# Layer 0's feed-forward with both residual streams in DRAM and its down sums added there by accumulating DMAs

## The chip, the cores and the metric

The kernel runs on one core of one Trainium2 chip. The metric is the device time of one execution in microseconds (us); the median of three plain runs before the change is 3101.7 us. A core has TensorE (PE, matrix products into PSUM), VectorE (DVE), ScalarE (ACT), GpSimd (POOL) and SyncE (SP, which here only issues DMAs), each working through its own instructions in order, and 16 DMA engines that they share. "PEld" is PE's loading of weights.

## The reference

Two layers act on two streams of 256 tokens by 2048 channels in float32: a latent stream `h` and a context stream `hc`. Layer 0 mixes by centred pooling, layer 1 by neighbourhood attention; each is followed by a gated feed-forward of width 5504. What matters here is layer 0, where both streams are updated:

```python
def conv_ffn(u, w_gate, w_up, conv_w, conv_b, w_down):
    T = u.shape[1]
    gp = jnp.pad(u @ w_gate, ((0, 0), (1, 1), (0, 0)))
    gte = gp[:, :T] * conv_w[0] + gp[:, 1:T + 1] * conv_w[1] + gp[:, 2:] * conv_w[2] + conv_b
    return (jax.nn.silu(gte) * (u @ w_up)) @ w_down
...
        h = h + ml[:, 2] * y_lat
        h = h + ml[:, 5] * conv_ffn(modulate(rms_norm(h, norm2_g[i]), ml[:, 3], ml[:, 4]),
                                    ffn_w_gate[i], ffn_w_up[i], ffn_conv_w[i], ffn_conv_b[i], ffn_w_down[i])
        if not last:
            hc = hc + mc[2] * y_ctx
            hc = hc + mc[5] * conv_ffn(modulate(rms_norm(hc, norm2_g[i]), mc[3], mc[4]),
                                       ffn_w_gate[i], ffn_w_up[i], ffn_conv_w[i], ffn_conv_b[i], ffn_w_down[i])
```

`ml` and `mc` are per-layer shifts, scales and gates, products of `silu(c)` and `silu(c_ctx)` with `w_mod`.

## The kernel before

**Layout.** Channels stand on the 128 partitions: a stream is 16 tiles (`KT`) of 128 channels by 256 tokens (`T`). The latent stream is `hl`, which lives for the whole kernel; the context stream is `hc`, 16 KB per partition, which lives until layer 0 ends. Each product is taken in three passes with the operands split in a high and a low part: ACT makes the high part (L143), DVE subtracts (L145), and PE runs hi x hi, hi x lo and lo x hi over 512 columns, both streams side by side.

**Mixer, up to some 455 us.** `mixer(g)` handles four tiles of channels. POOL adds the mixed result into `hl` and `hc` (L493); after group `g` these tiles of the streams are final until the feed-forward's own sums. The layer's modulation weights `wm` go through PE here (L193) in six slots, and the first eight feed-forward columns are computed group by group (`partial`, weights `wcg` and `wcu`).

**Feed-forward of layer 0, some 455 to 1694 us.** The 43 hidden tiles form eleven groups (`chunks`) of four, the last of three. For a hidden tile `f`, `gu0(f)` is 2 x 48 products over weights `wg_f` and `wu_f` (each loaded in two halves of 512 KB), and `gate0` makes the activation. For a group `c`, `down0(c)` is 16 tiles of 12 products each into the PSUM banks with tag "d" (three, and one with tag "m"); it follows the gate/up products of the next group. ACT scales each result by the gate into a buffer `dy` (L669, once for each stream) and POOL adds it to the stream (L670). Only in the last group DVE adds it, and the norm of the next layer is gathered there. Weights come by SP: three slots of 512 KB, then four pairs of high and low parts, so a half is asked for some seven halves ahead of its use. Between them SP loads layer 1's modulation weights (L219, L223), on which DVE works beside (`mod_pairs`, L241) in three slots of their own.

**Order.** Tiles come from pools, and a tile's reuse waits for its earlier readers. The framework orders each engine's instructions by a timeline that it simulates while it builds the program, so an edit can move instructions far from where it is written. Instructions on one engine, DMAs on SP's and on POOL's queue included, run in that order: one that waits holds up all behind it.

Of the kernel before, what the change touches and what calls it, by code (L numbers as in the profile page):

```python
# [10 lines left out]
F32 = mybir.dt.float32  # L11
F32R = mybir.dt.float32r
AF = mybir.ActivationFunctionType
ALU = mybir.AluOpType
# [3 lines left out]
P = 128  # L18
D = 2048
KT = D // P  # L20
T = 256
# [36 lines left out]
def kernel(ctx: ExitStack, tc: tile.TileContext, xT, cxT, wmod, wg, wu, wd, wp,  # L58
                         wq, wv, wo, vec, cc, rope, inv, strips, out):
    nc = tc.nc  # L60
# [8 lines left out]
    def bank(tag, name):  # L69

        if tag == "d" and nbank[0] is not None:
            nbank[0] += 1
            if nbank[0] % 4 == 0:
                tag = "m"
        return pp.tile([P, 512], F32, tag=tag, bufs={"gu": 4, "d": 3, "m": 1}[tag], name=name)

    def flat(a):
        return a.rearrange("p s t -> p (s t)")
# [5 lines left out]
    def V(name):  # L84
        a, b = _OFF[name]
        return vt[:, a:b]
# [11 lines left out]
    hl = main.tile([P, KT, T], F32, name="hl")  # L98
# [50 lines left out]
    def ld(src, name, share=0):  # L149
        return split(load(lambda a, b: src[:, a:b], 2048, name), name, share)  # L150
# [4 lines left out]
    both = (0, 1)  # L155
# [105 lines left out]
    def M(l, which, k, s):  # L261
        return modT[l, which * 4 + k // 4][:, k % 4, s : s + 1]
# [41 lines left out]
    def normalise(l, which, h_of, streams, rstd, pool, ks=range(KT), keep=A):  # L304

        for k in ks:
            a = ap0.tile([P, 2, 2, T], F32R, tag=f"A{k}", name=f"A{k}_{l}_{which}")
            y = pool.tile([P, 2, T], F32, tag="t2", name=f"nrm{l}{which}{k}")
            for s in streams:
                nc.vector.scalar_tensor_tensor(y[:, s], h_of(s)[:, k, :], M(l, which + 1, k, s),  # L310
                                               rstd[:, T * s : T * s + T], op0=ALU.mult, op1=ALU.mult)
                nc.scalar.activation(a[:, 0, s, :], y[:, s], AF.Identity, bias=M(l, which, k, s))
                ins = nc.vector.scalar_tensor_tensor(a[:, 1, s, :], y[:, s], M(l, which, k, s),
                                                     a[:, 0, s, :].bitcast(F32), op0=ALU.add, op1=ALU.subtract)
            keep[k] = a
            if l == 1 and k == 1:
                hold[:] = [ins.ins]

    chunks = [list(range(f, min(f + 4, NF))) for f in range(0, NF, 4)]
# [3 lines left out]
    with ExitStack() as ph0:  # L323
        p0 = ph0.enter_context(tc.tile_pool(name="p0", bufs=1, reuse_waits="tile"))
        f0 = ph0.enter_context(tc.tile_pool(name="f0", bufs=6, reuse_waits="tile"))
        hc = p0.tile([P, KT, T], F32, name="hc")

        quad = p0.tile([P, 4, 32], F32, name="quad")
        nc.vector.tensor_reduce(out=quad[:, 0], in_=ident.rearrange("p (j c) -> p c j", j=4), axis=AX.X, op=ALU.add)
# [2 lines left out]
        quad = flat(quad)  # L332

        def h_of(s):
            return hc if s else hl

        def act_tile(name, dt):
            return f0.tile([P, 2, 512], dt, tag="act", bufs=7, name=name)
# [23 lines left out]
        def gate0(f, pg, pu):  # L362
            g1 = f0.tile([P, 2, T], F32, tag="t2", name=f"g1_{f}")
            nc.scalar.activation(flat(g1), pg, AF.Identity, scale=V("cw1_0")[:, f : f + 1], bias=V("cb_0")[:, f : f + 1])
            pg3 = pg.rearrange("p (s t) -> p s t", s=2)
            nc.vector.scalar_tensor_tensor(g1[:, :, 1:T], pg3[:, :, 0 : T - 1], V("cw0_0")[:, f : f + 1],
                                           g1[:, :, 1:T], op0=ALU.mult, op1=ALU.add)
            nc.vector.scalar_tensor_tensor(g1[:, :, 0 : T - 1], pg3[:, :, 1:T], V("cw2_0")[:, f : f + 1],
                                           g1[:, :, 0 : T - 1], op0=ALU.mult, op1=ALU.add)
            sg = f0.tile([P, 512], F32, tag="t2", name=f"sg_{f}")  # L370
            nc.scalar.activation(sg, flat(g1), AF.Silu)
            nc.vector.tensor_tensor(sg, sg, pu, op=ALU.mult)
            if f == NS - 1:
                a = mp.tile([P, 2, 512], F32R, tag="macc", bufs=1, name=f"act_{f}")
            else:
                a = act_tile(f"act_{f}", F32R)
            a = [a[:, 0], a[:, 1]]
            nc.scalar.copy(a[0], sg)
            nc.vector.tensor_tensor(a[1], sg, a[0].bitcast(F32), op=ALU.subtract)
            return a, sg  # L380
# [5 lines left out]
        with ExitStack() as phs:  # L386
            st = phs.enter_context(tc.tile_pool(name="st", bufs=2, reuse_waits="tile"))
            for g in range(4):
                nc.sync.dma_start(hl[:, 4 * g : 4 * g + 4, :], xT[:, 4 * g : 4 * g + 4, :])
                nc.sync.dma_start(hc[:, 4 * g : 4 * g + 4, :], cxT[:, 4 * g : 4 * g + 4, :])  # L390
            n1 = Norm(both, f0, "n1")
            for k in range(KT):
                n1.add(h_of, k)
# [226 lines left out]
        def gu0(f):  # L620
            res = []
            for nm, wsrc in (("g", wg), ("u", wu)):
                parts = ld(wsrc[0, f], f"w{nm}0_{f}")
                if f > NS + 3:
                    next(pump, None)
                ps = bank("gu", f"{nm}0_{f}")
                for k in range(KT):
                    hi, lo = parts[k // 8]
                    c = P * (k % 8)
                    xh, xl = flat(A[k][:, 0]), flat(A[k][:, 1])  # L630
                    nc.tensor.matmul(ps, hi[:, c : c + P], xh, start=(k == 0), stop=False)  # L631
                    nc.tensor.matmul(ps, hi[:, c : c + P], xl, start=False, stop=False)  # L632
                    nc.tensor.matmul(ps, lo[:, c : c + P], xh, start=False, stop=(k == KT - 1))  # L633
                    if k == 7 and f > NS + 3:
                        next(pump, None)
                res.append(ps)
            return res
# [3 lines left out]
        def down0(c, fs, acts, after=None):  # L641
            n = len(fs)
            last = c == len(chunks) - 1
            for mg in range(4):
                parts = split(load(lambda a, b: wd[0, mg, :, fs[0] + a // 512 : fs[0] + b // 512, :], 512 * n, f"wd0_{c}_{mg}"),
                              f"wd0_{c}_{mg}")
                if c > 1:
                    next(pump, None)
                for m in range(4):
                    if m == 2 and c > 1:  # L650
                        next(pump, None)
                    ps = bank("d", f"d0_{c}_{mg}_{m}")
                    for i in range(n):
                        hi, lo = parts[i // 2]
                        o = 512 * (i % 2) + P * m
                        xh, xl = acts[i]
                        nc.tensor.matmul(ps, hi[:, o : o + P], xh, start=(i == 0), stop=False)  # L657
                        nc.tensor.matmul(ps, hi[:, o : o + P], xl, start=False, stop=False)  # L658
                        nc.tensor.matmul(ps, lo[:, o : o + P], xh, start=False, stop=(i == n - 1))  # L659
                    k = 4 * mg + m  # L660
                    if last:
                        for s in both:
                            nc.vector.scalar_tensor_tensor(h_of(s)[:, k, :], ps[:, T * s : T * s + T], M(0, 5, k, s),
                                                           h_of(s)[:, k, :], op0=ALU.mult, op1=ALU.add)
                        n3.add(h_of, k)
                    else:
                        y = f0.tile([P, 2, T], F32, tag="t2", name=f"dy{c}_{k}")
                        for s in both:
                            nc.scalar.activation(y[:, s], ps[:, T * s : T * s + T], AF.Copy, scale=M(0, 5, k, s))  # L669
                            nc.gpsimd.tensor_tensor(h_of(s)[:, k, :], h_of(s)[:, k, :], y[:, s], op=ALU.add)  # L670
                if after is not None:
                    after()
# [2 lines left out]
        normalise(0, 3, h_of, both, rstd, f0, range(12, 14))  # L675
        acts[NC], sg = gate0(NC, *r6)
        normalise(0, 3, h_of, both, rstd, f0, range(14, KT))
        res = gu0(NS)
        rest = [e for e in range(NS) if e not in acts]

# [5 lines left out]
        while rest and rest[0] < 4:  # L686
            more()
        down0(0, chunks[0], [acts[f] for f in chunks[0]], more)
        while rest:
            more()  # L690
        acts[NS], sg = gate0(NS, *res)
        for c, fs in enumerate(chunks):
            if c < 2:
                continue
            fs = [f for f in fs if f > NS]
            for f in fs:
                acts[f], sg = gate0(f, *gu0(f))
            down0(c - 1, chunks[c - 1], [acts[f] for f in chunks[c - 1]])
        prev = (len(chunks) - 1, chunks[-1], [acts[f] for f in chunks[-1]])
        down0(*prev)  # L700
        for _ in pump:
            pass
# [529 lines left out]
```

## Time and profile before

| what | value |
|---|---|
| median of three plain runs | 3101.7 us (3101.54 to 3102.39) |
| the profiled execution | 3103.48 us, its span 3101.7 us |
| granted TensorE clock over the span | 0.993 |
| DMA | 559.70 MB, 180 GB/s over the span |
| written to DRAM | 2.10 MB |

The profile is of one execution. Its page gives the busy time of each engine, the chain of work that ended last, followed back from the last instruction to whatever released each step, and groups of instructions by line, operation and tile: busy time, mean time of one, and the idle time of the engine just before them with what ended it. Other views list waits, instructions in order of time, and busy time by stretches. PE's products overlap, so the duration of one (0.395 us) is longer than the distance from one to the next.

### The profile page before, as it was taken

What the parts mean: (1) busy time and instruction counts of PE and PEld (TensorE: products, weight loads), DVE (VectorE), ACT (ScalarE), POOL (GpSimd) and SP (SyncE); (2) the same over time, 40 slices, a digit from 0 to 9 for tenths busy, and PEclk for the clock granted to TensorE, in tenths of its full rate; (3) what the DMA queues carried; (4) which work ended last, traced back from release to release, by engine and by line L of the source; (5) the groups of instructions that cost most, each with busy time, mean ns of one, the idle gap of its engine ahead of it and who ended that gap; (6) DMA issues with size and microseconds to landing.
All of it is one profiled execution on the core that took longest, in us unless ns stands there. A gap on an engine that the chain in (4) does not pass through costs nothing.

```text
span 3101.7 us, 40819 instructions
## 1 busy us (share of the span) xinstructions
PE 3030.0 (98%) x15082; PEld 2414.3 (78%) x15082; DVE 1932.6 (62%) x2748; ACT 1373.2 (44%) x2219; POOL 826.1 (27%) x823
## 2 busy tenths in 40 slices
PE   6999899999999999999999999999999999999998
PEld 2565558888888888888888788878788888888887
DVE  4445674285765848567485665564777666666666
ACT  3333454333233332323334444343545666656665
POOL 2011213213031230302213000000002466556665
PEclk9999999999999999999999999999999999999999
DMA  9978573264846657475573333332345565555563
GB/s 376 333 271 306 177 246 102 89 217 149 251 141 206 198 162 247 133 225 171 182 226 118 102 113 106 102 114 96 111 153 179 177 196 188 192 189 185 179 195 117
DMA packets 177927, 559.70 MB, mean 180 GB/s; under 512 B 17600, under 2 KB 22208, under 8 KB 177728
## 3 DMA queue, kind: packets, MB, share of 16 engines
q1 hardware_dynamic: 177728, 557.10, 55.0%
q8 instruction: 119, 1.95, 0.3%
q14 instruction: 80, 0.66, 0.1%
HBM read 554.93 MB, written 2.10 MB: 180 GB/s over the span
## 4 chain that ended last, share of the span: by engine, by line
PE 94%; DMA 2%; DVE 2%; POOL 1%; ACT 1%; issue 0%; SPq 0%; DVEq 0%; ACTq 0%; POOLq 0%
PE g L766 5%; PE u L766 5%; PE d L657 5%; PE d L659 5%; PE d L658 5%; PE d L813 4%; PE u L631 4%; PE u L632 4%; PE u L633 4%; PE g L631 4%; PE g L633 4%; PE g L632 4%; PE mod L193 3%; PE u L769 3%; PE g L769 3%; PE d L817 2%
## 5 line engine op out<-in xcount | busy, mean ns | idle before, releaser
L670 POOL TENSOR_TENSOR hl<-hl,dy 128x256 f32<-128x256 f32 x160 | 149.0, 931 | 958.6 <-ACT dy L669 957.3
L828 POOL TENSOR_TENSOR hl<-hl,dy 128x256 f32<-128x256 f32 x320 | 331.5, 1069 | 188.4 <-ACT dy L826 186.1
L241 DVE SCALAR_TENSOR_TENSOR macc<-wm,sc,macc 128x512 f32<-128x512 f32 (+1 forms) x360 | 325.2, 935 | 68.6 <-DMA wm<-wmod 67.6
L669 ACT ACTIVATE dy<-d,modT 128x256 f32<-128x256 f32 x320 | 133.5, 470 | 196.8 <-PE d L659 195.5
L193 PE MATMUL mod<-wm,sc 128*32 128x512 f32 x768 | 134.6, 618 | 26.6 <-DMA wm<-wmod 26.5
L670 POOL TENSOR_TENSOR hc<-hc,dy 128x256 f32<-128x256 f32 x160 | 126.0, 787 | 0.0
L145 DVE TENSOR_TENSOR wd_2l<-wd,wd_2h 128x1024 fp32r<-128x1024 f32 (+1 forms) x44 | 53.9, 1229 | 112.8 <-ACT wd_2h L143 112.8
L826 ACT ACTIVATE dy<-d,modT 128x512 f32<-128x512 f32 x160 | 104.4, 683 | 42.7 <-PE d L817 41.2
L915 POOL TENSOR_TENSOR rk<-rk,rp 128x256 f32<-128x256 f32 x16 | 13.2, 826 | 365.4 <-DVE rk L914 309.8
L145 DVE TENSOR_TENSOR wd_3l<-wd,wd_3h 128x1024 fp32r<-128x1024 f32 (+1 forms) x44 | 52.0, 1202 | 80.6 <-ACT wd_3h L143 80.6
L145 DVE TENSOR_TENSOR wd_1l<-wd,wd_1h 128x1024 fp32r<-128x1024 f32 (+1 forms) x44 | 53.7, 1224 | 58.6 <-ACT wd_1h L143 58.6
L466 POOL TENSOR_TENSOR pf<-ws,inv 128x256 f32<-128x256 f32 x32 | 27.7, 886 | 222.4 <-DVE ws L461 154.7
L193 PEld LDWEIGHTS mod<-wm,sc 128*32 128x32 f32 x768 | 23.6, 110 | 81.0 <-issue 59.4
L143 ACT CAST wd_1h<-wd 128x1024 fp32r<-128x1024 f32 (+1 forms) x44 | 45.2, 1029 | 79.8 <-PE u L632 50.6
L145 DVE TENSOR_TENSOR wd_0l<-wd,wd_0h 128x1024 fp32r<-128x1024 f32 (+1 forms) x44 | 54.6, 1247 | 40.7 <-ACT wd_0h L143 40.6
L1004 ACT ACTIVATE sb<-sb,nm 128x512 f32<-128x512 f32 x64 | 46.1, 721 | 64.4 <-DVE nm L1000 63.2
L143 ACT CAST wd_0h<-wd 128x1024 fp32r<-128x1024 f32 (+1 forms) x44 | 45.3, 1031 | 57.9 <-PE u L766 29.1
L792 DVE TENSOR_TENSOR actb<-sgb,actb 128x256 fp32r<-128x256 f32 x43 | 52.3, 1216 | 27.0 <-ACT actb L791 27.0
L657 PE MATMUL d<-act,wd_2h 128*128 128x512 f32 x172 | 68.0, 395 | 0.0
L658 PE MATMUL d<-act,wd_2h 128*128 128x512 f32 x172 | 67.9, 395 | 0.0
L657 PE MATMUL d<-act,wd_3h 128*128 128x512 f32 x172 | 67.9, 395 | 0.0
L657 PE MATMUL d<-act,wd_0h 128*128 128x512 f32 x172 | 67.9, 395 | 0.0
(1752 smaller groups left out, 9286.1 us busy)
## 6 DMA issues: line engine op xcount, KB each, us to landing
wm<-wmod SPq DMA_DIRECT2D x384, 512.0 KB, 6.1
wd<-wd SPq DMA_DIRECT2D x168, 512.0 KB, 4.4
wg<-wg SPq DMA_DIRECT2D x156, 512.0 KB, 4.6
wu<-wu SPq DMA_DIRECT2D x156, 512.0 KB, 4.5
wv<-wv SPq DMA_DIRECT2D x32, 512.0 KB, 3.9
wk<-wq SPq DMA_DIRECT2D x32, 512.0 KB, 4.0
wq<-wq SPq DMA_DIRECT2D x32, 512.0 KB, 3.7
wo<-wo SPq DMA_DIRECT2D x32, 512.0 KB, 4.4
```

The lines of the kernel that those rows point to most:

```text
L145: eng.tensor_tensor(lo[:, :n], t[:, :n], hi[:, :n].bitcast(F32), op=ALU.subtract)
L193: nc.tensor.matmul(ps[32 * j : 32 * j + 32, :], sc[:, 4 * g + j, :], ts[j // 2][0][:, 512 * (j % 2) : 512 * (j % 2) + 512], start=(g == 0) ...
L241: nc.vector.scalar_tensor_tensor(acc[s], v, sc2[:, k, s : s + 1], acc[s], op0=ALU.mult, op1=ALU.add)
L631: nc.tensor.matmul(ps, hi[:, c : c + P], xh, start=(k == 0), stop=False)
L632: nc.tensor.matmul(ps, hi[:, c : c + P], xl, start=False, stop=False)
L633: nc.tensor.matmul(ps, lo[:, c : c + P], xh, start=False, stop=(k == KT - 1))
L657: nc.tensor.matmul(ps, hi[:, o : o + P], xh, start=(i == 0), stop=False)
L658: nc.tensor.matmul(ps, hi[:, o : o + P], xl, start=False, stop=False)
L670: nc.gpsimd.tensor_tensor(h_of(s)[:, k, :], h_of(s)[:, k, :], y[:, s], op=ALU.add)
L766: nc.tensor.matmul(ps, hi[:, c : c + P], flat(B[k]), start=(k == 0), stop=False)
L769: nc.tensor.matmul(ps[:, T:], lo[:, c : c + P], B[k][:, 0], start=False, stop=(k == KT - 1))
L828: nc.gpsimd.tensor_tensor(hl[:, k, :], hl[:, k, :], y[:, q], op=ALU.add)
```

## The change

- A DRAM tile `hd` holds both streams. `moved(True)`, in the program after the second norm, stores `hl` and `hc` there by eight DMAs of 512 KB on SP's queue.
- The room of `hc` is then used as `dys`, eight slots of one down tile of both streams each (256 KB).
- In `down0` of groups 0 to 8, ACT writes the scaled results to a slot of `dys`, and in place of POOL's two adds one DMA on POOL's queue adds the slot to `hd` in DRAM: 144 such DMAs, each of 256 rows of 1 KB.
- After the gate of hidden tile 40 the room becomes a context stream again (`hc2`), and `moved(False)` loads both streams back by eight DMAs of 512 KB. Groups 9 and 10 are added on chip as before.

```diff
+        dr = ph0.enter_context(tc.tile_pool(name="dr", bufs=1, space=bass.MemoryType.DRAM))
+
+        hd = dr.tile([P, 2, KT, T], F32, name="hd")
+        CTX = [p0.tile([P, KT, T], F32, tag="hc", name="hc")]
...
         def h_of(s):
-            return hc if s else hl
+            return CTX[0] if s else hl
...
+                    elif away:
+                        y = away[0][:, 2 * (k % 8) : 2 * (k % 8) + 2, :]
+                        for s in both:
+                            nc.scalar.activation(y[:, s], ps[:, T * s : T * s + T], AF.Copy, scale=M(0, 5, k, s))
+                        nc.gpsimd.dma_start(out=hd[:, :, k, :], in_=y, accum_op=ALU.add)
                     else:
                         y = f0.tile([P, 2, T], F32, tag="t2", name=f"dy{c}_{k}")
...
         normalise(0, 3, h_of, both, rstd, f0, range(14, KT))
+
+        def moved(out_):
+            for g in range(0, KT, 4):
+                for s in both:
+                    x, y = hd[:, s, g : g + 4, :], h_of(s)[:, g : g + 4, :]
+                    if out_:
+                        nc.sync.dma_start(x, y)
+                    else:
+                        nc.sync.dma_start(y, x)
+
+        moved(True)
+        away = [p0.tile([P, KT, T], F32, tag="hc", name="dys")]
         res = gu0(NS)
...
                 acts[f], sg = gate0(f, *gu0(f))
+                if f == fs[0] and c == len(chunks) - 1:
+                    away.clear()
+                    CTX[0] = p0.tile([P, KT, T], F32, tag="hc", name="hc2")
+                    moved(False)
             down0(c - 1, chunks[c - 1], [acts[f] for f in chunks[c - 1]])
```

Three places in the order of the instructions. The first is SP's queue near the end of the mixer's stage, with modulation weights `wm_15` and `wm_20` of layer 0 and hidden weights `wcu`. Before:

```order
L127 DMA wm_15_2_1024_2845<-wmod 128x1024
L127 DMA wm_15_3_0_2865<-wmod 128x1024
L127 DMA wm_15_3_1024_2867<-wmod 128x1024
L127 DMA wm_20_1_0_2951<-wmod 128x1024
L127 DMA wm_20_1_1024_2953<-wmod 128x1024
```

And in the changed kernel, at the same place:

```order
L127 DMA wm_15_2_1024_2848<-wmod 128x1024
L692 DMA hd<-hl 128x1024
L127 DMA wm_15_3_0_2868<-wmod 128x1024
L127 DMA wm_15_3_1024_2870<-wmod 128x1024
L692 DMA hd<-hc 128x1024
L127 DMA wm_20_1_0_2954<-wmod 128x1024
L127 DMA wm_20_1_1024_2956<-wmod 128x1024
```

The stores of the last four tiles of each stream stand ahead of loads of modulation weights; the other three pairs stand in the same way after their mixer groups.

The second place is SP's queue around the ninth group's down products, with the weights of hidden tiles 40 and 41 and the modulation weights of layer 1 (`wm_7`, `wm_22`). Before:

```order
L127 DMA wd_8_3_1024_11732<-wd 128x1024
L127 DMA wg_40_0_11827<-wg 128x1024
L127 DMA wg_40_1024_11829<-wg 128x1024
L127 DMA wu_40_0_11915<-wu 128x1024
L127 DMA wu_40_1024_11917<-wu 128x1024
L127 DMA wg_41_0_11998<-wg 128x1024
L219 DMA wm_7_3_11885<-wmod 128x1024
L127 DMA wg_41_1024_12000<-wg 128x1024
L127 DMA wu_41_0_12071<-wu 128x1024
L219 DMA wm_7_4_11927<-wmod 128x1024
L127 DMA wu_41_1024_12073<-wu 128x1024
```

And in the changed kernel, from `wu_40` on:

```order
L127 DMA wu_40_0_11639<-wu 128x1024
L694 DMA hl<-hd 128x1024
L127 DMA wu_40_1024_11641<-wu 128x1024
L127 DMA wg_41_0_11731<-wg 128x1024
L694 DMA hl<-hd 128x1024
L127 DMA wg_41_1024_11733<-wg 128x1024
L127 DMA wu_41_0_11804<-wu 128x1024
L694 DMA hc_11722<-hd 128x1024 x3
L694 DMA hl<-hd 128x1024
L694 DMA hc_11722<-hd 128x1024
L127 DMA wu_41_1024_11806<-wu 128x1024
```

The reloads stand among the weights, five of them just ahead of the second half of `wu_41`; the loads of `wm_7` that stood here have moved ahead of `wg_40`. The reloads of `hl` each wait for the accumulations of their four tiles, the first of `hc` for all of the ninth group's.

The third place is the end of the mixer's stage on PE, around the last quarter of the products with `wm_15`. Before, these rows follow `wm_15_2_1024`:

```order
L289 MATMUL n2s<-ones,n2q_2749 128x1 x2
L545 MATMUL cg_0_2836<-Ad_2795,wcg_0h_2828 128x512
L545 MATMUL cg_1_2858<-Ad_2795,wcg_0h_2828 128x512
L193 MATMUL mod_15_2767<-wm_15_3_0_2865,sc 32x512 x2
L546 MATMUL cg_0_2836<-Ad_2795,wcg_0h_2828 128x512
```

In the changed kernel the same product stands behind twelve more:

```order
L549 MATMUL cg_1_2861<-Ad_2817,wcg_0h_2831 128x512
L550 MATMUL cg_1_2861<-Ad_2817,wcg_0l_2832 128x512
L548 MATMUL cg_0_2839<-Ad_2822,wcg_0h_2831 128x512
L548 MATMUL cg_1_2861<-Ad_2822,wcg_0h_2831 128x512
L193 MATMUL mod_15_2770<-wm_15_3_0_2868,sc 32x512 x2
L549 MATMUL cg_0_2839<-Ad_2822,wcg_0h_2831 128x512
```

What moved is only the place of the product with `wm_15_3_0`: the `cg` products that came after it now come ahead of it.

More of the change, by code (lines that the diff above doesn't have):

```diff
@@ L325 @@
         f0 = ph0.enter_context(tc.tile_pool(name="f0", bufs=6, reuse_waits="tile"))
-        hc = p0.tile([P, KT, T], F32, name="hc")
+        dr = ph0.enter_context(tc.tile_pool(name="dr", bufs=1, space=bass.MemoryType.DRAM))
+        hd = dr.tile([P, 2, KT, T], F32, name="hd")
+        CTX = [p0.tile([P, KT, T], F32, tag="hc", name="hc")]
         quad = p0.tile([P, 4, 32], F32, name="quad")
@@ L389 @@
                 nc.sync.dma_start(hl[:, 4 * g : 4 * g + 4, :], xT[:, 4 * g : 4 * g + 4, :])
-                nc.sync.dma_start(hc[:, 4 * g : 4 * g + 4, :], cxT[:, 4 * g : 4 * g + 4, :])
+                nc.sync.dma_start(CTX[0][:, 4 * g : 4 * g + 4, :], cxT[:, 4 * g : 4 * g + 4, :])
             n1 = Norm(both, f0, "n1")
```

## Prediction

> **What bounds the kernel now.** I read the page's first part and its chain first, then busy time by stage.
>
> ```profile
> PE 3030.0 (98%) x15082; PEld 2414.3 (78%) x15082; DVE 1932.6 (62%) x2748; ACT 1373.2 (44%) x2219; POOL 826.1 (27%) x823
> PE 94%; DMA 2%; DVE 2%; POOL 1%; ACT 1%; issue 0%; SPq 0%; DVEq 0%; ACTq 0%; POOLq 0%
> ```
>
> PE is busy for 98% of the span and makes up 94% of the chain that ended last; POOL, whose work the change takes away, makes up 1%. The stages (the columns are the stretch, its length, then busy time and instructions of each engine, the granted clock, the DMA share and GB/s):
>
> ```profile
> 0.00:30.00 30.00, 10.26 (x42) 4.78 (x42) 11.71 (x25) 12.11 (x34) 4.10 (x15) 1.00 0.92 345
> 30.00:455.00 425.00, 401.81 (x2142) 226.80 (x2141) 226.31 (x397) 164.33 (x299) 72.84 (x77) 0.98 0.79 285
> 455.00:1694.00 1239.00, 1239.00 (x5415) 1014.01 (x5414) 773.94 (x971) 448.26 (x698) 268.26 (x320) 1.00 0.56 176
> ...
> 770.00:847.00 77.00, 77.00 (x339) 63.29 (x339) 64.93 (x82) 21.60 (x25) 0.00 (x0) 1.00 0.83 259
> 847.00:924.00 77.00, 77.00 (x338) 62.89 (x337) 43.11 (x59) 30.07 (x50) 26.76 (x32) 1.00 0.41 130
> ...
> 1517.00:1562.00 45.00, 45.00 (x196) 36.51 (x195) 14.88 (x17) 21.02 (x39) 23.98 (x30) 1.00 0.30 99
> ```
>
> The stage that the change rewrites, layer 0's feed-forward from 455 to 1694 us, has PE busy for all of its 1239 us. A busy PE need not be at its peak, so I compare counts: 339 products in 77 us without any POOL work and with the DMA share at 0.83, 338 with 26.76 us of POOL work and the share at 0.41. So neither POOL's adds nor DMA traffic up to 0.83 changes PE's pace of 77/338 = 0.228 us for a product. There is nothing to win in this stage, only something to lose. What PE waited for in the two stages:
>
> ```profile
> PE g L631 <- DVE late L355: 0.9, 1, 0.9
> ...
> PE modt L203 <- ACT modev L198: 7.8, 7, 1.6
> PE mod L193 <- DMA wm<-wmod: 6.8, 11, 2.8
> PE pwu L528 <- DMA wcu<-wu: 5.4, 2, 4.1
> ```
>
> The first row is all that PE waited for from 455 to 1694 us (0.9 us, at its start); the other three are the largest waits of the mixer's stage, 30 to 455 us. There PE idled 425 - 401.8 = 23.2 us, of which 6.8 + 5.4 = 12.2 us were for loads. It is the only place where the new order could gain anything.
>
> **The adds on POOL go.** Nine groups by 16 tiles by two streams: 288 of these 320 instructions.
>
> ```profile
> L670 POOL TENSOR_TENSOR hl<-hl,dy 128x256 f32<-128x256 f32 x160 | 149.0, 931 | 958.6 <-ACT dy L669 957.3
> L670 POOL TENSOR_TENSOR hc<-hc,dy 128x256 f32<-128x256 f32 x160 | 126.0, 787 | 0.0
> L669 ACT ACTIVATE dy<-d,modT 128x256 f32<-128x256 f32 x320 | 133.5, 470 | 196.8 <-PE d L659 195.5
> ```
>
> That is 144 x (0.931 + 0.787) = 247 us of POOL time, but POOL idled 957 us there waiting for ACT, and ACT for PE. Gain on the path: **0**. ACT's two evictions per tile stay, into another buffer: 0.
>
> **The 144 accumulating DMAs.** No row shows one, so I bound the pace t, the time from the end of one to the end of the next.
>
> ```profile
> wd<-wd SPq DMA_DIRECT2D x168, 512.0 KB, 4.4
> wd<-wd SPq DMA_DIRECT2D x8, 256.0 KB, 2.7
> q1 hardware_dynamic: 177728, 557.10, 55.0%
> ```
>
> A load of 256 KB lands in 2.7 us and one of 512 KB in 4.4: 1.7 us for each 256 KB more, and 1.0 us that does not grow. From below, t = 1.7 us, if the add is free. From above by packets: 0.550 x 3101.7 x 16 / 177728 = 0.154 us of one engine for each packet of some 3 KB. The new DMA has 256 rows of 1 KB; if each row costs three packets (source read, destination read, write), t = 768 x 0.154 / 16 = 7.4 us; with two, 4.9. I take **3.4 us**, the 256 KB load's price with the bytes counted twice, as the row nearest to it.
>
> What t has to stay under: the pitch of the tiles.
>
> ```profile
> 1517.75 0.40 PE L657 MATMUL d<-act,wd_0h 128*128 128x512 f32 x1
> ...
> 1520.75 0.84 ACT L669 ACTIVATE dy<-d,modT 128x256 f32<-128x256 f32 x2 [1.97 <-PE d L659]
> 1523.55 0.84 ACT L669 ACTIVATE dy<-d,modT 128x256 f32<-128x256 f32 x2 [1.96 <-PE d L659]
> ```
>
> The ninth group's down product begins at 1517.75, and a tile is evicted every 2.80 us. POOL's queue then holds nothing but these DMAs, each waiting for its eviction and for the landing of the eighth before it; ACT waits for that same landing before it writes a slot again, and behind it stand the weight casts on which PE depends. The 16th tile, evicted at 1520.75 + 15 x 2.80 = 1562.8, needs the 8th DMA, done at 1521.6 + 8t + 1.0; the four banks of PSUM give three tiles more, 8.4 us. So ACT stops PE only when t > (1562.8 + 8.4 - 1522.6)/8 = **6.1 us**. At 3.4 us a group's DMAs are done 16 x 3.4 = 54 us after it begins, and the next begins at least 480 products (three gate/up pairs of 96 each and one down product) or 109 us after it. Cost: **0**. In bytes, a down product's 45 us have a DMA share of 0.30; 54 us of these DMAs spill over into the next products, where 0.83 cost PE nothing.
>
> **The eight reloads** stand in SP's queue (the order above). Those of the context stream wait for all of group 8's accumulations, and the second half of wu_41 stands behind them.
>
> ```profile
> 1572.83 0.33 SPq L127 DMA_DIRECT2D wu<-wu  x1
> ...
> L631 PE MATMUL u<-A,wu_41h x10: 389/392/404, 1595.6 to 1601.9; 128*128 128x512 f32 x10
> ...
> L143 ACT CAST wd_1h<-wd 128x1024 fp32r<-128x1024 f32 (+1 forms) x44 | 45.2, 1029 | 79.8 <-PE u L632 50.6
> L145 DVE TENSOR_TENSOR wd_2l<-wd,wd_2h 128x1024 fp32r<-128x1024 f32 (+1 forms) x44 | 53.9, 1229 | 112.8 <-ACT wd_2h L143 112.8
> ```
>
> Before, that half is issued at 1572.8. PE starts on wu_41 at 1595.6 and reaches its second half 24 products later, at 1601.1. Counting back: 1.03 + 1.23 us for cast and subtraction, 4.4 for its landing, 5 x 1.7 for the five reloads ahead of it: SP must be let go by 1585.9. The last accumulation is done at 1522.6 + 16t, so the reloads hide while t < **3.96 us**; at 3.4 that is 1577, 9 us in time. Cost: **0**. This is the narrowest place of the change.
>
> **The layer 1 modulation loads** move ahead of some feed-forward weights, and DVE's multiply-adds with them, into the down products. There DVE is busy 14.9 of 45 us, so it has room: 0.
>
> **The eight stores** do not stand where the code has them: the scheduler put a pair into SP's queue after each mixer group, among loads that PE is short of.
>
> ```profile
> SPq L127 <- PE mod L193: 200.0, 76, 16.1
> ...
> 164.36 1.06 SPq L127 DMA_DIRECT2D wcu<-wu  x2
> 171.63 11.10 SPq L127 DMA_DIRECT2D wm<-wmod  x8
> ...
> 170.28 1.25 POOL L493 TENSOR_TENSOR hc<-hc,pz 128x256 f32<-128x256 f32 x1
> ...
> 349.16 1.33 POOL L493 TENSOR_TENSOR hl<-hl,pz 128x256 f32<-128x256 f32 x1 [1.03 <-ACT pz L491]
> ...
> 349.90 3.21 SPq L127 DMA_DIRECT2D wm<-wmod  x4
> ...
> 355.72 1.05 PE L193 MATMUL mod<-wm,sc 128*32 128x512 f32 x4
> ```
>
> From 30 to 470 us SP itself waited 200 us for PE to free a slot, so most loads are asked for early. At the second pair, for example, SP stood still until 171.6 anyway, and the adds that the store waits for end at 171.5. The fourth pair is tight: wm_15_3_0 was issued at 349.9 and used at 355.7, 5.8 us later. Now a store stands ahead of it that waits for the add ending at 350.5; with 0.4 us per issue the load goes out at 351.3 behind 1.7 us of store, and lands at 351.3 + 5.8 + 1.7 = 358.8. PE's new order takes 12 products and one small sum more before it, 12 x 0.228 + 0.3 = 3.0 us, and needs it at 358.7. So close to nothing is lost; I take **+1 us**. The bounds for this stage: -12.2 us, if the new order removes every wait for loads, and 8 x 1.7 = +13.6 us, if every store delays PE in full.
>
> **Sum:** 0 + 0 + 0 + 0 + 1 = +1 us. The profiled execution took 3103.48 us around its span of 3101.70; the median of the plain runs, 3101.7, lies 1.8 us below it. I add the sum to the median: **3103 us**.
>
> **A rule against this change.** One of the nine adds that POOL did between 1519 and 1533 us took 1.34 us and the others 0.73 to 0.75, so something holds POOL up beside DVE's work.
>
> ```profile
> 1521.36 0.74 POOL L670 TENSOR_TENSOR hl<-hl,dy 128x256 f32<-128x256 f32 x1 [87.87 <-ACT dy L669]
> 1530.48 1.34 POOL L670 TENSOR_TENSOR hl<-hl,dy 128x256 f32<-128x256 f32 x1 [2.08 <-ACT dy L669]
> ```
>
> The Trainium skill, page "SBUF — State Buffer", section "SBUF: two separate sides", says that GpSimd itself builds the descriptors of a DMA it issues, and cannot write them while a VectorE instruction holds the port pair that both share; it gives 620 ns alone against about 3100 ns. No run so far shows this for a DMA. As a mechanism of this kernel it is rival 2.
>
> **Rivals.** (1) **The accumulations are slow**, on the other side of my forecast. Between 3.96 and 6.1 us a piece, the loss comes once, at the reloads: 16 x (t - 3.96), so 3118 us at 4.9. Above 6.1 each group loses 8 x (t - 6.1) as well: at 7.4, 55 + 9 x 10.4 = 149 us and 3252. For it: rows of 1 KB, where the queue's packets now hold 557.1 MB / 177728 = 3.1 KB, and a destination that must be read first. Against it: the down products' low DMA share, and eight slots. 0.12. (2) **DVE holds POOL up**: if every accumulating DMA has to sit out one of DVE's subtractions, t = 3.4 + 1.23 = 4.6 us, over the reloads' 3.96, and the time is 3103 + 16 x 0.64 = 3113. For it: the 1.34 us above. Against it: eight of nine adds were not held up, and DVE is idle for two thirds of a down product. 0.06. (3) **The stores decide in the mixer's stage**: DMA share 0.79, and up to +13.6 us, 3115. Against it: SP's 200 us of waiting for PE. 0.08. (4) **The new order in the mixer's stage gains**: up to 12.2 us, 3090. For it: the wcu waits at its end depend on the order of loads. Against it: the same products and more bytes. 0.08. (5) **The change doesn't do what it says for the time**: POOL is freed, and nothing waited for POOL. That is the forecast itself, 0.66, with its own range 3097 to 3109.
>
> **How the numbers follow.** A measurement of this kernel can tell about 0.2%, 6 us, from no change. Faster by more is rival 4: 0.08. Within it is the forecast: 0.66. Slower by more is rivals 1, 2 and 3: 0.12 + 0.06 + 0.08 = 0.26. The range goes from rival 4's 3090 to 3120, past the bounds of rivals 2 and 3 and rival 1 at 4.9 us; what is left out is a slower accumulation.
>
> **What would show it.** PE still busy for the whole of the feed-forward at 338 products per 77 us; ACT's evictions waiting for PE and not for a DMA; the landing of an accumulating DMA under some 5 us, and the last of group 8 by 1577; the reloads ending before the second half of wu_41 is due; PE's idle time before 455 us within a few us of 23.2. The forecast fails if the accumulating DMAs come at more than 3.96 us each, if they hold up the weight loads on the same engines, or if PE idles anew around 350 to 390 us.

## The result and the profile after

The changed kernel took 3119.5 us (median of four, 3118.5 to 3120.9), the kernel before beside it 3102.1 us: a ratio of 1.0054, with a 95% interval of 1.0037 to 1.0072. It is slower by some 17 us, more than the 0.2% that can be told from no change. The two profiled executions differ by 15.0 us in their spans, 3116.7 against 3101.7, and the readings below are of these.

The page of the changed kernel, its busy times and the chain; then busy time by stage (stretch, length, then PE's busy time with its instructions, clock, DMA share, GB/s):

```profile
PE 3044.5 (98%) x15082; PEld 2417.6 (78%) x15082; DVE 1920.0 (62%) x2748; ACT 1372.2 (44%) x2219; POOL 736.6 (24%) x679
PE 93%; DMA 2%; DVE 1%; POOL 1%; ACT 1%; issue 1%; SPq 0%; DVEq 0%; ACTq 0%; POOLq 0%
```

```profile
30.00:455.00 425.00, 399.70 (x2073) 0.98 0.79 282
455.00:1694.00 1239.00, 1238.12 (x5414) 1.00 0.78 213
```

The feed-forward, which the change rewrites, runs as before: 5414 instructions of PE in 1239 us against 5415, although the DMA share rose from 0.56 to 0.78. The mixer's stage, which the change does not touch in its text, is where PE does less: 2073 instructions in the same 425 us instead of 2142, while its idle time hardly moved, 25.3 us against 23.2. The same point of the program shows it in two places: the sums of the second norm, late in the mixer's stage, and those of the third, at the end of the feed-forward. Rows of these two tiles (min, median and max duration in ns, first and last start), before and then after:

```profile
L289 PE MATMUL n2s<-ones,n2acc x8: 164/250/250, 353.8 to 354.5; 128*128 128x1 f32 x8
...
L289 PE MATMUL n3s<-ones,n3q x16: 250/250/271, 1709.9 to 1711.6; 128*128 128x1 f32 x16
```

```profile
L289 PE MATMUL n2s<-ones,n2acc x8: 164/250/250, 369.0 to 369.7; 128*128 128x1 f32 x8
...
L289 PE MATMUL n3s<-ones,n3q x16: 250/352/353, 1725.4 to 1728.3; 128*128 128x1 f32 x16
```

The changed kernel is 15.2 us late at the first and 15.5 us at the second. Nearly all of the loss is made before the first, none of it among the accumulations. What PE waited for there did not grow by that much:

```profile
PE modt L203 <- ACT modev L198: 10.3, 9, 1.8
PE mod L193 <- DMA wm<-wmod: 6.9, 9, 2.8
PE pwu L531 <- DMA wcu<-wu: 4.8, 2, 3.5
```

Waits for loads went from 12.2 to 11.7 us, those for the modulation's eviction from 7.8 to 10.3. So PE was not held up; it was busy for longer, 3044.5 us against 3030.0, with the same 15082 instructions. One group holds most of that. The modulation products of layer 0 in the groups of instructions, before and then after (count, busy us, mean ns, idle time before):

```profile
L193 PE MATMUL mod<-wm,sc 128*32 128x512 f32 x768 | 134.6, 618 | 26.6 <-DMA wm<-wmod 26.5
```

```profile
L193 PE MATMUL mod<-wm,sc 128*32 128x512 f32 x768 | 143.6, 626 | 25.4 <-DMA wm<-wmod 25.4
```

The same 768 records (384 products, two records each) take 9.0 us more. The timeline shows how. Four products, the strips, fill 32 of the array's 128 columns each; strips 0 and 1 read the first half of a load of weights, strips 2 and 3 the second half. One such group of four, first as it runs in the kernel before, then its first half in the changed kernel (start, duration):

```profile
97.51 0.40 PE L547 MATMUL cg<-Ad,wcg_0l 128*128 128x512 f32 x1
97.84 1.06 PE L193 MATMUL mod<-wm,sc 128*32 128x512 f32 x8
98.84 0.50 PE L545 MATMUL cg<-Ad,wcg_0h 128*128 128x512 f32 x1
99.18 0.40 PE L546 MATMUL cg<-Ad,wcg_0h 128*128 128x512 f32 x1
99.42 0.40 PE L547 MATMUL cg<-Ad,wcg_0l 128*128 128x512 f32 x1
```

```profile
98.21 0.39 PE L548 MATMUL cg<-Ad,wcg_0h 128*128 128x512 f32 x1
98.53 1.05 PE L193 MATMUL mod<-wm,sc 128*32 128x512 f32 x4
99.51 0.50 PE L549 MATMUL cg<-Ad,wcg_0h 128*128 128x512 f32 x1
99.85 0.39 PE L550 MATMUL cg<-Ad,wcg_0l 128*128 128x512 f32 x1
...
100.61 0.62 PE L193 MATMUL mod<-wm,sc 128*32 128x512 f32 x2
100.62 0.63 PE L531 MATMUL pwu<-wcu,sh 128*32 128x256 f32 x4
```

Four strips take 98.84 - 97.84 = 1.00 us until the next product starts; two strips take 99.51 - 98.53 = 0.98 us. Strips that follow each other run side by side, so two cost as much as four. The Trainium skill, page "TensorE: Matmul & The Clock Gate", section "Part 3: Packing small matmuls — row/col tiling", puts the span of such a pack at one product's duration and about 4 ns for each further tile. This trace agrees in kind: two further strips add 0.02 us, 1.00 against 0.98, where an estimate from the page's figure is 2 x 0.004 = 0.008. Around a run there is more: the steps into it (97.51 to 97.84) and out of it (98.84 to 99.18) take 0.33 and 0.34 us, where one product follows another in 0.24 (99.18 to 99.42). So a group in two halves costs about 0.98 + 0.09 + 0.10 = 1.2 us more than a group in one piece, when full-width products stand between. By PE's order, 27 of the 96 groups were in pieces before the change and 35 after it; eight more at 1.2 us would be 9.6 us, an estimate, beside the 9.0 of the row.

The accumulations themselves, in the changed kernel's queues (packets, MB, share of 16 engines), groups and issues (the last number of the third row is the median from issue to landing in us):

```profile
q0 software_dynamic: 39168, 37.76, 8.1%
...
L673 POOL DMA_DIRECT2D hd<-dys x144 | 157.0, 1094 | 959.3 <-ACT dys L672 959.3
...
hd<-dys POOLq DMA_DIRECT2D x144, 256.0 KB, 8.0
```

POOL waited for ACT alone. One accumulation used 0.081 x 3116.7 x 16 / 144 = 28 us of engine time, 1.75 us if spread over 16 engines, in 39168 / 144 = 272 packets.

### The profile page after: what moved, and what is told of

Read it like the earlier page. It is cut to its first block, busy times and chain, and to the rows that moved or that the text cites. A ratio compares the mean times of both kernels' runs of the same rounds, so it can differ in the third digit from the quotient of the medians.

```text
span 3116.7 us, 40674 instructions
## 1 busy us (share of the span) xinstructions
PE 3044.5 (98%) x15082; PEld 2417.6 (78%) x15082; DVE 1920.0 (62%) x2748; ACT 1372.2 (44%) x2219; POOL 736.6 (24%) x679
## 3 DMA queue, kind: packets, MB, share of 16 engines
q0 software_dynamic: 39168, 37.76, 8.1%
## 4 chain that ended last, share of the span: by engine, by line
PE 93%; DMA 2%; DVE 1%; POOL 1%; ACT 1%; issue 1%; SPq 0%; DVEq 0%; ACTq 0%; POOLq 0%
PE g L790 5%; PE u L790 5%; PE d L660 5%; PE d L662 5%; PE d L661 5%; PE d L837 4%; PE g L634 4%; PE u L634 4%; PE u L635 4%; PE u L636 4%; PE g L636 4%; PE g L635 4%; PE mod L193 3%; PE u L793 3%; PE g L793 3%; PE d L841 2%
## 5 line engine op out<-in xcount | busy, mean ns | idle before, releaser
L673 POOL DMA_DIRECT2D hd<-dys x144 | 157.0, 1094 | 959.3 <-ACT dys L672 959.3
L852 POOL TENSOR_TENSOR hl<-hl,dy 128x256 f32<-128x256 f32 x320 | 330.5, 1066 | 188.4 <-ACT dy L850 186.1
L241 DVE SCALAR_TENSOR_TENSOR macc<-wm,sc,macc 128x512 f32<-128x512 f32 (+1 forms) x360 | 318.0, 925 | 70.6 <-DMA wm<-wmod 69.5
L672 ACT ACTIVATE dys<-d,modT 128x256 f32<-128x256 f32 x288 | 120.4, 470 | 187.4 <-PE d L662 94.7
L193 PE MATMUL mod<-wm,sc 128*32 128x512 f32 x768 | 143.6, 626 | 25.4 <-DMA wm<-wmod 25.4
L145 DVE TENSOR_TENSOR wd_2l<-wd,wd_2h 128x1024 fp32r<-128x1024 f32 (+1 forms) x44 | 53.6, 1221 | 55.4 <-ACT wd_2h L143 55.4
L374 ACT ACTIVATE sg<-g 128x512 f32<-128x512 f32 x43 | 27.2, 632 | 130.7 <-DVE g L371 130.7
L145 DVE TENSOR_TENSOR wd_1l<-wd,wd_1h 128x1024 fp32r<-128x1024 f32 (+1 forms) x44 | 53.6, 1222 | 32.5 <-ACT wd_1h L143 32.5
L662 PE MATMUL d<-act,wd_2l 128*128 128x512 f32 x172 | 67.9, 395 | 0.0
```

The lines of the kernel that those rows point to most:

```text
L145: eng.tensor_tensor(lo[:, :n], t[:, :n], hi[:, :n].bitcast(F32), op=ALU.subtract)
L193: nc.tensor.matmul(ps[32 * j : 32 * j + 32, :], sc[:, 4 * g + j, :], ts[j // 2][0][:, 512 * (j % 2) : 512 * (j % 2) + 512], start=(g == 0) ...
L241: nc.vector.scalar_tensor_tensor(acc[s], v, sc2[:, k, s : s + 1], acc[s], op0=ALU.mult, op1=ALU.add)
L852: nc.gpsimd.tensor_tensor(hl[:, k, :], hl[:, k, :], y[:, q], op=ALU.add)
```

## The experiments

Theory A: the eight stores made the scheduler order PE's products in the mixer's stage otherwise, and the order costs the time. Theory B: the stores themselves cost it, by their bytes and by what they hold up on SP. Theory C: the accumulations or the reloads cost it.

**1. Stores late.** The changed kernel, the stores queued behind the loads of `wu_8`:

```diff
-        moved(True)
-        away = [p0.tile([P, KT, T], F32, tag="hc", name="dys")]
         res = gu0(NS)
+        with tc.issue_after(last_load[0]):
+            moved(True)
+        away = [p0.tile([P, KT, T], F32, tag="hc", name="dys")]
```

> The changed kernel, with the eight stores queued behind the loads of wu_8, so that they stand in the first gate/up product of the feed-forward and not in the mixer's stage; PE's order up to 455 us is then row for row that of the kernel before. Accumulations, reloads and the freed context buffer stay. Theory A (the stores made the scheduler choose another order of PE's products in the mixer's stage, with the two halves of the modulation products apart): the 15 us are gone, 3102 to 3107. Theory B (the stores themselves, their bytes and SP's waits, cost 8 x 1.7 = 13.6 us): they now stand ahead of the first loads of wd, and the cost moves with them, 3108 to 3116. Theory C (the accumulations or the reloads cost it in the feed-forward): as the changed kernel, 3119.

Measured 3099.9 us, a ratio to the kernel before of 1.0001 (0.9992 to 1.0010). That is 2 us under Theory A's range and far from those of B and C; the loss is gone with all accumulations and reloads in place, so C falls. Eight stores of 512 KB ahead of the feed-forward's loads cost nothing either.

**2. Stores alone.** The kernel before, with this ahead of `gu0(NS)`, and `hd` allocated in DRAM:

```diff
+        for g in range(0, KT, 4):
+            for s in both:
+                nc.sync.dma_start(hd[:, s, g : g + 4, :], h_of(s)[:, g : g + 4, :])
         res = gu0(NS)
```

> The kernel before with the eight stores alone added, where the changed kernel has them; the sums stay on chip and are added by POOL, and nothing reads what is stored. PE's order in the mixer's stage is that of the changed kernel. Theory A (order): 3115 to 3120, with 47 runs of four records of L193 instead of 32. Theory B (stores): the same time, but as idle time of PE before loads, some 14 us more of it than in the kernel before. Theory C (accumulations): 3102.

Measured 3117.1 us, 1.0056 (1.0044 to 1.0069): the whole loss without an accumulation. Its row of modulation products reads as the changed kernel's:

```profile
L193 PE MATMUL mod<-wm,sc 128*32 128x512 f32 x768 | 143.7, 624 | 26.3 <-DMA wm<-wmod 26.2
```

Busy for 143.7 us against 134.6, idle as before: that fits A and not B. But stores and order came together here. Experiments 5 and 6 separate them.

**3 and 4. Halves held together by a critical section**, in the kernel before and in the changed kernel:

```diff
-            for j in range(4):
-                nc.tensor.matmul(ps[32 * j : 32 * j + 32, :], sc[:, 4 * g + j, :],
...
+            with tc.tile_critical():
+                for j in range(4):
+                    nc.tensor.matmul(ps[32 * j : 32 * j + 32, :], sc[:, 4 * g + j, :],
```

> The kernel before, with the four strips of each modulation product of the mixer's stage (two products from each half of the weights) scheduled as one piece, so that nothing stands between the halves. Theory A: a run of four records takes as long as one of eight, about 1.05 us, so the 32 lone halves in the kernel before (16 pairs) give back 16 x 1.0 = 16 us, less what PE now waits longer for the second halves: 3082 to 3092. If the separation of the halves costs nothing (A wrong): 3100 to 3104, or more if PE waits for the second halves.

> The changed kernel, stores where it has them, with the four strips of each modulation product scheduled as one piece. Theory A: the order no longer differs where it costs, so the time is within 6 us of the same edit in the kernel before, 3082 to 3096, and 24 us or more under the changed kernel. Theory B (stores) or C (accumulations): 14 to 17 us above the same edit in the kernel before.

Measured 3438.4 and 3461.5 us, 1.109 and 1.116 times the kernel before. Both are far outside what was expected, and say nothing about strips. What PE waited for in the first of them (total us, times, longest):

```profile
PE mod L194 <- DMA wm<-wmod: 127.3, 36, 6.4
PE mod L194 <- DMA inv<-inv: 49.8, 2, 41.3
...
PE mod L194 <- ACT pad L456: 12.9, 4, 5.9
```

PE's modulation products wait here for a load of `inv` and for ACT's padding, which they do not read. The atomic piece brought waits of its own.

**5 and 6. The order alone, and the stores without it.** PE's 1650 products of the mixer's stage are chained in a given order: `ORDER` lists them as runs of places in the program's text, and an edge between neighbours sets the order alone. In experiment 5 the kernel before gets the changed kernel's order, in 6 the changed kernel that of before:

```diff
+ORDER = [(9, 4), (0, 8), (13, 8), (8, 1), (21, 50), (81, 9), (93, 7), (71, 4), (90, 1), (75, 2), (91, 2),
...
             need(97)
+            pe = [i for i in nc.cur_bb.bb.instructions if "Matm" in type(i).__name__]
+            pe = [pe[a + k] for a, n in ORDER for k in range(n)]
+            for x, y in zip(pe, pe[1:]):
+                tc.add_manual_dep(y, x.name, mybir.DependencyInfo(mybir.DependencyClass.NoSync,
+                                                                  mybir.DependencyReason.DATA), reason="order")
```

> The kernel before, without stores or accumulations, with PE's 1650 products of the mixer's stage chained in the order that the changed kernel has there (a list of their places; the chain sets the order alone and adds no wait). Theory A (that order costs it): 3114 to 3120, with 97 runs of L193 as in the changed kernel. Theory B (the stores' bytes and SP's waits cost it): 3098 to 3103, as the kernel before.

> The changed kernel, with its stores among the mixer's loads, its accumulations and its reloads, and PE's products of the mixer's stage chained in the order of the kernel before. Theory A: 3098 to 3106, the loss is gone although every store stands where it stood. Theory B: 3112 to 3119, with some 14 us more idle time of PE before loads than in the kernel before.

The order alone: 3119.8 us, 1.0057 (1.0044 to 1.0070). The changed kernel without it: 3105.8 us, 1.0014 (1.0005 to 1.0023). Their rows, of 5 and then of 6:

```profile
L231 PE MATMUL mod<-wm,sc 128*32 128x512 f32 x768 | 144.6, 630 | 25.3 <-DMA wm<-wmod 25.2
```

```profile
L228 PE MATMUL mod<-wm,sc 128*32 128x512 f32 x768 | 134.2, 621 | 26.9 <-DMA wm<-wmod 26.9
```

In the traces PE takes the modulation products of the mixer's stage in 97 runs in experiment 5, as in the changed kernel, and in 89 in experiment 6, as in the kernel before. The first gives the whole loss without a store, the second leaves 0.05 to 0.23%, 2 to 7 us, with every store in the mixer's stage. So A holds, and B is worth a few us at most. What those are is open: the profiled execution of experiment 6 has a span of 3101.3 us, under that of the kernel before, and shows nothing of them; and no run chains the kernel before in its own order, so they may also be the price of the chain.

**7 and 8. Halves joined**, by the same chain. `ORDER` is the kernel's own, with the earlier strips of each group in pieces moved down to its last one: 27 groups in the kernel before, 35 in the changed kernel.

> The kernel before, PE's products of the mixer's stage chained in its own order with one thing changed: where a modulation product's four strips are not next to each other (27 of its 96 groups), the earlier ones are moved down to the last one. Theory A with its price: a run of four records takes 1.01 us and one of eight 1.09 us, and each entry costs 0.08 us, so each group gives back 1.01 us: 27 us, 3073, and 3070 to 3085 with some of it lost to slots of weights that come free later. If a separation costs nothing: 3098 to 3104.

> The changed kernel, PE's products of the mixer's stage chained in its own order, with the earlier strips moved down to the last one in the 35 groups where they are apart. Theory A: 35 x 1.01 = 35 us under the changed kernel, 3084, and no more than 10 us above the same edit in the kernel before. Theory B: it stays some 14 us or more above that.

Measured 3080.8 us, 0.9931 (0.9918 to 0.9943), and 3085.8 us, 0.9954 (0.9941 to 0.9966). Both are faster than either kernel. The row of 7:

```profile
L224 PE MATMUL mod<-wm,sc 128*32 128x512 f32 x768 | 110.1, 611 | 27.4 <-DMA wm<-wmod 27.4
```

134.6 - 110.1 = 24.5 us less busy, with the idle time before it 0.8 us up. The time fell by 21.3 us, 0.79 us for each group joined instead of 1.01, perhaps because some pieces had stood among the strips of `pwg` or `pwu`, which start beside them (100.61 and 100.62 in the timeline above); that was not tried apart. The changed kernel fell by 34 us, 0.96 for each of 35.

**9. More halves apart.** The kernel before in its own order, with the later strips of 13 more groups moved down past three other products; 40 groups are then in pieces.

> The kernel before, PE's products of the mixer's stage chained in its own order with the opposite edit: in 13 more of the 96 groups (40 in all) the strips of the second half of the weights are moved down past three other products, so that they are apart. Theory A: the price is linear. No group apart took 3080.8 and 27 apart 3102.1 us, 0.79 us each; 13 more give 3102 + 13 x 0.79 = 3112, or 3115 at the 1.01 us of the runs' lengths. If the gain of the joined orders came from something else that the edit moved: 3100 to 3105.

Measured 3115.5 us, 1.0044 (1.0032 to 1.0057), as A expected. The row has gone up by 11.0 us:

```profile
L231 PE MATMUL mod<-wm,sc 128*32 128x512 f32 x768 | 145.6, 621 | 25.4 <-DMA wm<-wmod 25.4
```

No group in pieces, 27 and 40 give 3081, 3102 and 3115 us: 0.8 us for each of the first 27, and 14.8 / 13 = 1.1 us, against the kernel before that ran beside it, for each of the others.

**10. Accumulations doubled**, to size the margin of the step that I had called narrowest. The kernel of experiment 1, and:

```diff
-                        y = away[0][:, 2 * (k % 8) : 2 * (k % 8) + 2, :]
+                        y = away[0][:, 2 * (k % 7) : 2 * (k % 7) + 2, :]
...
                         nc.gpsimd.dma_start(out=hd[:, :, k, :], in_=y, accum_op=ALU.add)
+                        nc.gpsimd.dma_start(out=hd[:, :, (k + 8) % KT, :], in_=away[0][:, 14:16, :], accum_op=ALU.add)
...
+        nc.gpsimd.memset(away[0][:, 14:16, :], 0.0)
```

> The changed kernel with late stores (experiment 1), and a second accumulating DMA of 256 KB behind each of the 144, which adds zeros eight tiles away; the sums have seven slots instead of eight, since one holds the zeros. By the records of the changed kernel (8.1% of 16 engines x 3116.7 us / 144 = 28 us of engine time, 1.75 us on all 16) a tile's two take 3.5 us: behind the 2.8 us pitch by 0.7 us a tile, but done 56 us after a group begins, under the 3.96 us of the reloads, so no change: 3098 to 3106. By the 3.4 us that was forecast a tile's two take 6.8 us, over what ACT can wait for with seven slots, (1562.8 + 8.4 - 1522.6) / 9 = 5.4 us: each of nine groups loses 9 x 1.4 = 13 us and the reloads 16 x 2.8 = 45 us, 3260.

Measured 3120.4 us, 1.0064 (1.0050 to 1.0078): neither. The ninth group's first and last accumulation of sums in POOL's timeline, and the first one of zeros between them:

```profile
1527.31 1.09 POOL L674 DMA_DIRECT2D hd<-dys  x1 [55.60 <-ACT dys L673]
...
1533.92 1.09 POOL L675 DMA_DIRECT2D hd<-dys  x1 [2.72 <-DMA hd<-dys]
...
1576.26 1.09 POOL L674 DMA_DIRECT2D hd<-dys  x1 [0.55 <-ACT wg_41h L144]
```

POOL issues 24 accumulations from the first to the last of them, 16 of sums and 8 of zeros (the other 8 of zeros had gone out before): (1576.26 - 1527.31) / 23 = 2.13 us for each, waits included. So the 3.4 us of the forecast is too long, and the 1.75 of the records is not contradicted. Yet there was a cost, which the waits of the feed-forward show:

```profile
POOL hd L675 <- DMA hd<-dys: 362.5, 115, 9.0
...
ACT dys L673 <- DMA hd<-dys: 53.6, 22, 5.8
...
PE u L637 <- DVE wu_42l L146: 2.7, 2, 2.0
PE g L637 <- DVE wg_42l L146: 1.9, 1, 1.9
PE u L637 <- DVE wu_18l L146: 1.8, 1, 1.8
```

ACT now waits 53.6 us for slots. PE waits up to 2.0 us at a time, mostly for weights split late, and 12.5 us in all between 440 and 1700 us, where it waited 0.9 in experiment 1. POOL waits too, as it does not in the changed kernel: the accumulations of zeros stood 362.5 us in its queue until an earlier accumulation had landed (the one issued at 1527.31 lets go of that at 1533.92), and the sums behind them stood still as well. So this experiment brought a wait of its own beside the doubled traffic and the lost slot, and the DMA share of the feed-forward was 0.95; which of these made the weights late was not tried apart. What I had wrong is the landing, "t + 1.0 us". For the sums it was, here and then in the changed kernel,

```profile
DMA to landing us min/median/max: 4.0/9.9/18.0
```

```profile
DMA to landing us min/median/max: 4.1/8.0/12.4
```

A slot comes round after 7 x 2.8 = 19.6 us here, which a landing of up to 18.0 and the wait in POOL's queue fill; in the changed kernel it has 8 x 2.8 = 22.4 us for 12.4.

**11. Late stores and joined halves**: experiment 1 with the order of experiment 7.

> The changed kernel with late stores (experiment 1) and the joined order of experiment 7 in the mixer's stage. Theory A: nothing of the change costs time then, so as experiment 7: 3078 to 3083, and 3 to 5 us under experiment 8, whose stores stand in the mixer's stage. If the stores cost the same 3 to 5 us wherever they stand: 3084 to 3086.

Measured 3077.7 us, 0.9924 (0.9912 to 0.9937), the same as experiment 7 within the intervals. It is 8 us under experiment 8, more than the 3 to 5 expected; the two differ in their joined orders as well as in the place of the stores, so the 8 us cannot be put down to the stores alone. With its stores late the change costs nothing and gains nothing; what gains is the order.

## Why the prediction was right and wrong

The time fell inside the range, at its upper edge, but the likeliest case, within 0.2%, did not come. That the range held is luck: its upper part was made for slow accumulations, a POOL held up by DVE, or stores that make PE wait, and none of these is what happened. By its steps:

- **What bounds the kernel**: right. PE bounds it, and neither POOL's adds nor a DMA share of 0.78 changed PE's pace in the feed-forward. Removing 247 us of POOL's work gained nothing.
- **The accumulations, 0**: right for the time. The pace of 3.4 us was twice too long: 1.75 us by the records, close to the lower bound of 1.7 that I left for the nearest row's price with the bytes counted twice. The upper bounds took two or three packets for each of the 256 rows; there are 272 in all, about one for each. The landing was far longer than I expected of it, "under some 5 us": 8.0. The two errors did not matter at eight slots; the kernel of experiment 10, with twice the traffic, seven slots and POOL's own waits, was some 20 us slower than that of experiment 1.
- **The reloads, 0**: right. SP's queue shows the first three of the context stream issued together:

```profile
1589.02 1.27 SPq L694 DMA_DIRECT2D hc<-hd  x3
```

  Less the 15.2 us by which the kernel is late, that is 1573.8, where I had said 1577 and needed 1585.9.
- **The moved modulation loads of layer 1, 0**: right; both kernels stay level through the feed-forward.
- **The eight stores, +1 us within -12.2 and +13.6**: the step that failed. For the stores as such it was near: 2 to 7 us in experiment 6. It failed where it went from waits to order. I looked at the new order for what it makes late, and priced it as "12 products and one small sum more before it, 12 x 0.228 + 0.3"; against a gain from the order I wrote "the same products and more bytes". Both take a product's price as fixed wherever it stands. It is not: four strips next to each other take 1.00 us, in two halves 2 x 0.98. And I priced one place of the order, where eight more groups had come apart in the whole stage. So the bounds, which priced waits and stores alone, did not hold the term either: it was 15 us and more.
- **Rival 3**, stores that decide in the mixer's stage, named the right stage and nearly the right time (3115), with the wrong mechanism: PE's waits for loads went from 12.2 to 11.7 us.
- **Rival 2** and the rule of the Trainium skill, page "SBUF — State Buffer", section "SBUF: two separate sides": not seen. All 144 issues took 1079 to 1580 ns, none the page's 3100 ns, and the 98 of them that ran beside an instruction of DVE have the same median, 1088 ns, as the others. (In experiment 10 issues reach 4818 ns, as the last of eight that followed one another without a wait, most of them some 0.53 us longer than the one before; that looks like a backlog of their own.) The row of the 144:

```profile
L673 POOL DMA_DIRECT2D hd<-dys x144: 1079/1088/1580, 500.4 to 1579.9; - x144
```

What carries the 15 us, then: 9.0 of PE's 14.5 us of added busy time are in the row of the strips, and the waits for `modev` add 2.5. PE's timeline can be taken step by step, from the start of one product to the start of the next, up to the first sum of the third norm. The modulation products stand there in 97 runs instead of 89. Idle time left out, the steps inside these runs, into them and out of them take 10.2 us more, the steps at the products `pwg`, `pwu`, `ptg` and `ptu` 2.6, all others 1.0, and idle time 3.0; that is 16.8 us, of which 1.3 are made up by a first product that starts earlier. So eight more runs cost 10.2 / 8 = 1.3 us each, near the 1.2 read off one group. The runs show that the order carries all of it together (experiment 5) and what pieces cost by themselves (7 and 9); the smaller shares were not tried apart.

## What to carry to other kernels

Where a scheduler orders the engines, look for where an edit moves the order of the engine that bounds the kernel, also in stages that the edit does not touch, and price an instruction by its neighbours: the rows of one line in runs of different length show whether company makes it free. Products on strips of the array belong next to each other; if their operands come by two loads, let the first wait for the second. An order can be tested alone, by chaining the instructions in it, and that tells it apart from traffic in two runs.

## What the runs showed of the hardware that was not expected

- Two 32-column products of 128x512 in fp32 take as long as four, 0.98 against 1.00 us, and a full-width product between them ends the sharing: 0.8 to 1.1 us for each group in pieces.
- The step into a run of strips takes 0.33 us and the step out of it 0.34 us, against 0.24 from one full-width product to the next.
- An accumulating DMA of 256 KB into DRAM takes 28 us of engine time (1.75 us on 16 engines) but lands after 8.0 us in the median, beside loads at a DMA share of 0.78, where a plain load of 256 KB lands after 2.8 in the same kernel (eight loads of `wd`).
